# Zero-row keys, transposed vector sums and operand addresses in a two-block transformer kernel

## The chip, the cores and the metric

The kernel runs on one core of a Trainium2 chip. The metric is the device time of one execution in microseconds; for the kernel before it is the median of three runs. Engines are named TensorE (PE in the profile, PEld for its weight loads), VectorE (DVE), ScalarE (ACT), GpSimd (POOL) and SyncE (SP, which issues most DMAs).

## The reference

256 tokens of width 1024 pass through two transformer blocks of two layers each. All arithmetic is float32. Cut to what matters here:

```python
def first_block(x, p, positions, w_in, ...):
    for i in range(2):
        q, k, v, qi, ki, wi, u, vs = split(x @ w_in[i], ...)
        a = dsa_attention(rope(q), rope(k), v, rope(qi), rope(ki), wi)  # 8 heads on 2 key heads of 64
        b = spatial_gating(gelu(u), gelu(vs), ...)
        x = layer_norm(ALPHA * x + concat(a, b) @ w_o[i], ...)
        gate, up = split(x @ w_ffn_in[i], 2)
        ffn = (silu(gate) * up) @ w_ffn_out[i]
        ple = (p[i] @ w_ple[i]) * sigmoid(x @ w_ple_gate[i])
        x = layer_norm(ALPHA * x + ffn + ple, ...)
    return x

def second_block(x, c, positions, ada_w, ada_b, ...):
    cond = silu(c)                                            # one vector of 1024
    for layer in range(2):
        sh1, sc1, g1, sh2, sc2, g2 = split(cond @ ada_w[layer] + ada_b[layer], 6)
        h = rms_norm(x, norm_mix[layer]) * (1 + sc1) + sh1
        # layer 0: MLA (8 heads of 64 + 32) and dilated windows (3 groups of 4 heads of 64)
        # layer 1: differential attention (4 heads of 2 x 64) and MoBA (8 heads of 64)
        x = x + g1 * mixer(h, ...)
        h = rms_norm(x, norm_mlp[layer]) * (1 + sc2) + sh2
        x = x + g2 * (relu(h @ mlp_w1[layer]) ** 2 @ mlp_w2[layer])
    return x
```

In dsa_attention a small index attention (4 heads of 64) chooses which keys of each query row count.

## The kernel before

**Tiling.** The tokens are two halves of 128, numbered rr = 0 and 1, one token to a partition. Weights stream from HBM in units of 128 partitions x 1024 floats. SP issues the loads in order into ring "w" of six buffers (`load_unit`, L396). Each unit is split into a high part h (ScalarE, L407) and the remainder l (VectorE, L408), both in a format of fewer bits, fp32r; a float32 product is then three fp32r matmuls: high by high, high by low, low by high. While the feed-forwards run, the split parts also go into mix, qTa and kTa, tiles that attention uses at other times.

**Three forms of product.** `product` (L436 to L438) keeps a 128x128 block of x stationary and moves 512 columns of weights (384 or 336 in some projections), for one half. `joint_product` (L457 to L459), the first part of the feed-forwards, keeps a 128x128 block of weights stationary and moves 256 columns of x, both halves at once; it has 1,152 matmuls for each of its three lines, 832 of them with weights in the ring and 320 with weights in mix, kTa or qTa. `joint_rows` (L472 to L474), the feed-forwards' second part, keeps blocks of the hidden state (hh and hl, one for each half) stationary and moves 512 columns of weights. The split x lies in XH and XL.

**Scores.** `scores` (L578 to L594) first writes a mask into a PSUM bank with an identity matmul (L587) and adds q times k (L593) for two heads, two instructions to each product, since plain float32 goes through in two. Query and key columns of two heads of 64 lie above each other in one 128-row block, in qTa or qTb and in a key tile: vaa for DSA, kTb for the dilated heads and MoBA, kTa for the differential heads and MLA. A head uses partitions 0 to 63 or 64 to 127 (`lo : lo + 64`) of both. MLA's heads have 96 rows and always begin at partition 0. There are 44 score calls on 64 rows: 16 of DSA, 12 dilated, 8 differential and 8 of MoBA, 208 instructions in the records of TensorE. The DSA index attention has 8 more matmul pairs of 64 rows (L778). Transposed heads come out of PSUM through `columns_of` and its callers, with one copy for up to four blocks, on ScalarE or, at L767, VectorE.

**Conditioning.** `conditioning` (L646) computes cond @ ada_w in 12 jobs. Each streams eight 128x1024 tiles through ring "w"; VectorE multiplies each by a column of cond and adds it up in acc (tag kTb; L656 for the first, L658 for the seven others). The sum over the 128 partitions remains. Four jobs (the gates) get it by a matmul with ones as rows. The other eight, called column jobs here, need it as columns of 128 and take eight float32 matmuls of one column (L676) and an addition (L680). The jobs run as fillers in the feed-forwards, between the joint matmuls.

**Addresses.** A tile's place in SBUF is a byte offset within each partition, given out pool by pool (const, ring, act). What matters below is that offset modulo 256: the ring's w, h and l are at 0, XH and XL at 0, qTa0 and qTa1 at 224, mix0, mix1 and kTa at 32, hid0, hh0 and hl0 at 32, hid1, hh1, hl1 and kTb at 128, hr0 and hr1 (a small input of the first block) at 160 and 224. SBUF is full.

**Order.** The Tile framework puts instructions into each engine's queue by priorities (PRIORITY) and estimated times, so a changed instruction can change the order around it.

Of the kernel before, what the change touches and what calls it, by code (L numbers as in the profile page):

```python
# [10 lines left out]
F32 = mybir.dt.float32  # L11
F32R = mybir.dt.float32r
BF16 = mybir.dt.bfloat16
I32 = mybir.dt.int32
# [8 lines left out]
NH = 2  # L23
# [55 lines left out]
def body(ctx: ExitStack, tc: tile.TileContext, I, out):  # L79
# [8 lines left out]
    act = pool("act", 1)  # L88
    psum = pool("psum", 1, space=bass.MemoryType.PSUM)
# [27 lines left out]
    def new(p, shape, tag, bufs, dt=F32):  # L117
        serial[0] += 1
        return p.tile(shape, dt, tag=tag, name=f"{tag}_{serial[0]}", bufs=bufs)
# [94 lines left out]
    def setup_second():  # L214
# [15 lines left out]
        G.iota(diff_i, pattern=[[-1, P]], base=0, channel_multiplier=1)  # L230
        strided = {}
# [262 lines left out]
    XH = act.tile([P, NH, KB, P], F32, tag="xh", name="xh", bufs=1)  # L494
    XL = act.tile([P, NH, KB, P], F32, tag="xl", name="xl", bufs=1)
# [150 lines left out]
    def conditioning():  # L646

        cond, ones, cols_a = C["cond"], C["ones"], C["cols_a"]
        for l, j in COND_JOBS:
# [23 lines left out]
            else:  # L673
                ps = bank("m", 0)
                for k in range(KB):
                    T.matmul(ps[:, k : k + 1], acc[:, k * P : (k + 1) * P], ones[:, 0:1],  # L676
                             start=True, stop=True)
                bcol = cols_a[:, l * 48 + j * 8 : l * 48 + j * 8 + 8]
                m = ctile([P, KB], f"mod{l}{name}")
                V.tensor_tensor(m, ps[:, :KB], bcol, op=ALU.add)  # L680
# [70 lines left out]

    @ranked("fin")
# [8 lines left out]
    def dsa_select(rr, row, wi, qT, kT, m4):  # L761
# [3 lines left out]
        def put(b0, ps3):  # L765
            A.copy(qT[:, 4:6], ps3[:, 0:2])
            V.tensor_copy(kT[:, 1, rr * P : rr * P + P], ps3[:, 2])  # L767
# [5 lines left out]
        for half in range(2):  # L773
            ps = bank("a", rr)
            p3 = ps[:, : 2 * nk].rearrange("p (h k) -> p h k", h=2)
            lo = half * 64
            for j in range(2):
                T.matmul(p3[:, j], qT[lo : lo + 64, 4 + j], kT[lo : lo + 64, 1, :nk], start=True, stop=True)  # L778
# [19 lines left out]
    def dsa_heads(rr, qT, kT, va, mask, mix):  # L798
        nk = P * (rr + 1)
        for g in range(2):  # L800
            lo = g * 64
            po3 = None
            for j0 in (0, 2):
                p3 = scores([(qT[lo : lo + 64, j0 + j], kT[lo : lo + 64, 0, :nk]) for j in range(2)], rr,
                            [(0, mask)])
# [12 lines left out]
    def first_layer(l, rr):  # L818
        x = state["x"][rr]
        xs = transposed(rr, x, 8, kind="a")  # L820
        kT = params(("kT", l), lambda: new(act, [P, 2, S], "vaa", 1))
# [28 lines left out]
        def put(b0, ps3):  # L850
            if b0:
                A.copy(kT[:, 0, rr * P : rr * P + P], ps3[:, 0])
# [311 lines left out]
    def dilated(rr, rqs, qT, kT, va, mix):  # L1164
        nk = P * (rr + 1)
        for lo_h in range(2):
            lo = lo_h * 64
# [3 lines left out]
            for g in range(3):  # L1171
                far, diag = C["dil_masks"][g]
                masks = [(0, diag)] if rr == 0 else [(0, far), (P, diag)]
                p3 = scores([(qT[lo : lo + 64, 2 * g + h // 2], kT[lo : lo + 64, 2 * g + h // 2, :nk]) for h in hs],
                            rr, masks, "a" if g < 2 else "m")
# [21 lines left out]
    def even_layer(rr):  # L1197
# [14 lines left out]
        dkT = params(("dil_kT",), lambda: new(act, [P, 6, S], "kTb", 1))  # L1212
# [40 lines left out]
        to_columns(rr, dk, 6, dkT[:, :, rr * P : rr * P + P])  # L1253
# [7 lines left out]
    def diff(rr, rqs, qT, kT, va, mix):  # L1261
        nk = P * (rr + 1)
        po3 = None
        for h0 in (0, 2):
            sums = new(act, [P, 2, 2], "df_s", 2)
            pts = []
            for m in range(2):
                lo = m * 64
# [197 lines left out]
```

## Time and profile before

| what | value |
|---|---|
| device time, median of 3 runs (range) | 1335.47 us (1334.87 to 1335.48) |
| profiled execution: time, span of the trace | 1336.68 us, 1335.0 us |
| TensorE busy | 1303.6 us (98%), 8006 instructions |
| VectorE busy | 1011.1 us (76%), 2096 |
| ScalarE busy | 727.2 us (54%), 1488 |
| GpSimd busy | 38.6 us (3%), 99 |
| read from HBM | 267.60 MB, 201 GB/s over the span |

The times are from one execution recorded on the chip. "Busy" is the share of the span in which an engine has at least one instruction in work. Matmuls overlap in this record (each begins before the last one's recorded end), so a matmul's duration is not what it costs; the distance of start times, called its pitch below, is. The chain of waits follows the work that ended last back to what released it.

### The profile page before, as it was taken

Reading aid. Unit: us, or ns where it says so; the run is one execution under the profiler, and the core shown is the slowest. Engines: PE = TensorE matmul, PEld = TensorE weight load, DVE = VectorE, ACT = ScalarE, POOL = GpSimd, SP = SyncE. Lnnn points to the kernel's source line nnn. Section 1 sums busy time; section 2 is a strip of 40 time slices with the busy share of each in tenths; the row PEclk is TensorE's granted clock in tenths of the full one; section 3 lists DMA queues with packets and bytes.
Section 4 is the critical chain, followed back from the end, with each engine's and each line's share of the span. In section 5 each row is a group of like instructions: output and inputs, shape, how many; then the busy total and the mean of one; then the engine's idle time right before and its main releaser. Section 6 shows DMA issues by size and latency. Waiting matters only on the chain.

```text
span 1335.0 us, 21908 instructions
## 1 busy us (share of the span) xinstructions
PE 1303.6 (98%) x8006; PEld 1145.2 (86%) x8006; DVE 1011.1 (76%) x2096; ACT 727.2 (54%) x1488; POOL 38.6 (3%) x99
## 2 busy tenths in 40 slices
PE   7999999999999999999899998999999999999998
PEld 6788999998878799999798976998987777799896
DVE  7979888668878988577769867867677996865552
ACT  6554554343555454454567667655447675854541
POOL 2000000000000000000010000000001000000000
PEclk9999999999999999999999999999999999999999
DMA  8635898786654698587564444777765534565631
GB/s 283 212 128 172 301 325 287 247 292 233 178 174 143 190 330 307 183 304 256 157 167 121 146 154 146 232 238 244 236 232 142 178 111 143 174 203 184 185 107 48
DMA packets 121805, 270.10 MB, mean 202 GB/s; under 512 B 9587, under 2 KB 30160, under 8 KB 121696
## 3 DMA queue, kind: packets, MB, share of 16 engines
q1 hardware_dynamic: 120304, 265.62, 60.8%
q0 software_dynamic: 1392, 3.07, 1.1%
q8 instruction: 63, 1.03, 0.3%
q14 instruction: 46, 0.38, 0.1%
HBM read 267.60 MB, written 1.05 MB: 201 GB/s over the span
## 4 chain that ended last, share of the span: by engine, by line
PE 86%; DVE 7%; ACT 3%; DMA 2%; issue 2%; POOL 1%; SPq 0%; POOLq 0%; ACTq 0%; DVEq 0%
PE m L458 10%; PE m L459 10%; PE m L457 10%; PE m L436 7%; PE m L438 7%; PE m L437 7%; PE a L472 6%; PE a L473 6%; PE a L474 6%; PE a L593 3%; PE a L436 2%; PE a L437 2%; PE a L438 2%; DVE l L408 2%; PE a L628 1%
## 5 line engine op out<-in xcount | busy, mean ns | idle before, releaser
L407 ACT CAST h<-w 128x512 fp32r<-128x512 f32 (+3 forms) x634 | 354.4, 605 | 269.9 <-DMA w<-in_w_ffn_in 51.7
L408 DVE TENSOR_TENSOR l<-w,h 128x512 fp32r<-128x512 f32 (+3 forms) x634 | 401.5, 664 | 74.5 <-ACT h L407 73.7
L457 PE MATMUL m<-xh,h 128*128 128x256 f32 x832 | 235.9, 284 | 0.0
L458 PE MATMUL m<-xl,h 128*128 128x256 f32 x832 | 235.7, 283 | 0.0
L459 PE MATMUL m<-xh,l 128*128 128x256 f32 x832 | 235.5, 283 | 0.0
L436 PE MATMUL m<-h,xh 128*128 128x512 f32 (+3 forms) x544 | 208.2, 384 | 3.5 <-ACT h L407 2.9
L438 PE MATMUL m<-h,xl 128*128 128x512 f32 (+3 forms) x544 | 206.2, 381 | 4.6 <-DVE xl L1020 4.4
L437 PE MATMUL m<-l,xh 128*128 128x512 f32 (+3 forms) x544 | 205.7, 379 | 0.6 <-DVE l L408 0.4
L458 PEld LDWEIGHTS m<-xl,h 128*128 128x128 f32 x832 | 159.0, 191 | 0.4
L457 PEld LDWEIGHTS m<-xh,h 128*128 128x128 f32 x832 | 158.9, 191 | 0.3
L459 PEld LDWEIGHTS m<-xh,l 128*128 128x128 f32 x832 | 158.9, 191 | 0.3
L658 DVE SCALAR_TENSOR_TENSOR kTb<-w,cond,kTb 128x1024 f32<-128x1024 f32 x84 | 107.6, 1280 | 30.8 <-DMA w<-in_ada_w 30.2
L438 PEld LDWEIGHTS m<-h,xl 128*128 128x128 f32 x544 | 103.9, 191 | 20.1 <-DVE xl L1020 5.3
L436 PEld LDWEIGHTS m<-h,xh 128*128 128x128 f32 x544 | 104.4, 192 | 18.5 <-ACT h L407 3.6
L437 PEld LDWEIGHTS m<-l,xh 128*128 128x128 f32 x544 | 104.1, 191 | 14.1 <-DVE l L408 1.6
L472 PE MATMUL a<-h,hh 128*128 128x512 f32 x216 | 85.5, 396 | 0.0
L473 PE MATMUL a<-l,hh 128*128 128x512 f32 x216 | 85.4, 396 | 0.0
L474 PE MATMUL a<-h,hl 128*128 128x512 f32 x216 | 85.4, 395 | 0.0
L407 ACT CAST qTa<-w 128x512 fp32r<-128x512 f32 x60 | 34.4, 622 | 36.6 <-DMA w<-in_w_ffn_in 11.4
L407 ACT CAST kTa<-w 128x512 fp32r<-128x512 f32 x60 | 34.7, 626 | 33.2 <-PE m L459 7.4
L407 ACT CAST mix<-w 128x512 fp32r<-128x512 f32 x60 | 34.7, 620 | 30.7 <-DMA w<-in_w_ffn_in 8.5
L408 DVE TENSOR_TENSOR kTa<-w,kTa 128x512 fp32r<-128x512 f32 x60 | 39.0, 687 | 14.7 <-ACT kTa L407 14.7
(441 smaller groups left out, 2458.3 us busy)
## 6 DMA issues: line engine op xcount, KB each, us to landing
w<-in_mlp_w SPq DMA_DIRECT2D x128, 512.0 KB, 4.2
w<-in_ada_w SPq DMA_DIRECT2D x96, 512.0 KB, 4.8
w<-in_w_ffn_in SPq DMA_DIRECT2D x80, 512.0 KB, 5.1
w<-in_w_ffn_out SPq DMA_DIRECT2D x44, 512.0 KB, 5.4
w<-in_odd_w_in SPq DMA_DIRECT2D x24, 512.0 KB, 4.4
w<-in_even_w_in SPq DMA_DIRECT2D x24, 384.0 KB, 3.4
w<-in_w_in SPq DMA_DIRECT2D x16, 512.0 KB, 7.2
w<-in_w_o SPq DMA_DIRECT2D x16, 512.0 KB, 6.0
```

The source lines that it names most:

```text
L407: split = [A.copy(r(ht[:, c]), wt[:, c]), V.tensor_tensor(r(lt[:, c]), wt[:, c], ht[:, c], op=ALU.subtract)]
L408: V.tensor_tensor(r(lt[:, c]), wt[:, c], ht[:, c], op=ALU.subtract)]
L436: T.matmul(ps, r(xh), r(wh[:, cols]), start=first, stop=False)
L437: T.matmul(ps, r(xh), r(wl[:, cols]), start=False, stop=False)
L438: mm = T.matmul(ps, r(xl), r(wh[:, cols]), start=False, stop=last)
L457: T.matmul(ps, r(wh[:, cols]), r(XH[:, :, k]), start=first, stop=False)
L458: T.matmul(ps, r(wh[:, cols]), r(XL[:, :, k]), start=False, stop=False)
L459: T.matmul(ps, r(wl[:, cols]), r(XH[:, :, k]), start=False, stop=last)
L472: T.matmul(ps, r(xh), r(wh[:, cols]), start=start and k == 0, stop=False)
L473: T.matmul(ps, r(xh), r(wl[:, cols]), start=False, stop=False)
L474: T.matmul(ps, r(xl), r(wh[:, cols]), start=False, stop=False)
L658: V.scalar_tensor_tensor(acc, wt, cond[:, k : k + 1], acc, op0=ALU.mult, op1=ALU.add)
```

## The change

Three things are changed.

**Zero-row keys.** A key tile gets one block for each head instead of one for two heads. Each block holds the head's 64 rows on the partitions where they were and zeros on the other 64 (`zeroed_keys`, two GpSimd memsets for each tile), so q times k takes all 128 rows of both operands: the other head's query rows meet zeros. A key copy from PSUM becomes two, one for the lower and one for the upper 64 partitions (`to_keys`). vaa grows to [128, 4, 256], kTb to [128, 12, 256] for the dilated heads and [128, 8, 256] for MoBA, kTa's key tile to [128, 8, 256]; MLA's stay.

**Turned vector sums.** In a column job VectorE transposes acc in 32x32 blocks into a buffer of ring "w" and reduces each row over groups of 32 to 128x32. One float32 matmul with `quarters` (ones where row and column agree modulo 32) adds up the four groups of partitions, and four additions on 32 partitions each take the place of the one.

**Addresses.** Tiles of pool act whose size is not a multiple of 64 floats, and vaa and vab, go to a new pool "small", and XH and XL go to a new pool "last", behind a tile of 32 bytes. XH and XL then lie at 32 modulo 256, and the ring, hh, hl, hr, hid, mix, qTa and kTa at 0. The scratch for dynamic DMA descriptors shrinks from 16384 to 4096 bytes for each partition, which makes room for the larger tiles.

Context lines are cut to the nearest.

```diff
@@ -86,6 +86,8 @@
     act = pool("act", 1)
+    last = pool("last", 1)
+    small = pool("small", 1)
     psum = pool("psum", 1, space=bass.MemoryType.PSUM)
@@ -116,6 +118,9 @@
         serial[0] += 1
+        if p is act and (math.prod(shape[1:]) % 64 or tag in ("vaa", "vab")):
+            p = small
         return p.tile(shape, dt, tag=tag, name=f"{tag}_{serial[0]}", bufs=bufs)
@@ -228,6 +233,10 @@
         G.iota(diff_i, pattern=[[-1, P]], base=0, channel_multiplier=1)
+        quarters = C["quarters"] = ctile([P, P], "quarters")
+        rem = new(act, [P, P], "hid0", 2, I32)
+        V.tensor_single_scalar(rem, diff_i, 31, op=ALU.bitwise_and)
+        V.tensor_scalar(quarters, rem, 0, 1.0, op0=ALU.is_equal, op1=ALU.mult)
         strided = {}
@@ -491,8 +500,11 @@
-    XH = act.tile([P, NH, KB, P], F32, tag="xh", name="xh", bufs=1)
-    XL = act.tile([P, NH, KB, P], F32, tag="xl", name="xl", bufs=1)
+    apart = last.tile([P, 8], F32, tag="apart", name="apart", bufs=1)
+    V.memset(apart, 0.0)
+    XH = last.tile([P, NH, KB, P], F32, tag="xh", name="xh", bufs=1)
+    XL = last.tile([P, NH, KB, P], F32, tag="xl", name="xl", bufs=1)
@@ -671,13 +683,19 @@
             else:
+                turned = new(ring, [P, UNIT], "w", NW)
+                V.transpose(turned, acc)
+                part = new(act, [P, 32], "ada_q", 1)
+                V.tensor_reduce(out=part, in_=turned.rearrange("p (b k) -> p b k", k=32), op=ALU.add, axis=AX.X)
                 ps = bank("m", 0)
-                for k in range(KB):
-                    T.matmul(ps[:, k : k + 1], acc[:, k * P : (k + 1) * P], ones[:, 0:1],
-                             start=True, stop=True)
+                T.matmul(ps[:, 0:32], C["quarters"], part, start=True, stop=True)
                 bcol = cols_a[:, l * 48 + j * 8 : l * 48 + j * 8 + 8]
                 m = ctile([P, KB], f"mod{l}{name}")
-                V.tensor_tensor(m, ps[:, :KB], bcol, op=ALU.add)
+                for q in range(4):
+                    at_q = slice(32 * q, 32 * q + 32)
+                    V.tensor_tensor(m[at_q], ps[at_q, q:32:4], bcol[at_q], op=ALU.add)
                 if name[:2] == "sc":
@@ -749,6 +767,25 @@
+    def zeroed_keys(shape, tag):
+        kz = new(act, shape, tag, 1)
+        G.memset(kz[64:128, 0::2], 0.0)
+        G.memset(kz[0:64, 1::2], 0.0)
+        return kz
+    def to_keys(rr, row, nblk, kz):
+        here = slice(rr * P, rr * P + P)
+        def put(b0, ps3):
+            n = ps3.shape[1]
+            A.copy(kz[0:64, 2 * b0 : 2 * (b0 + n) : 2, here], ps3[0:64])
+            A.copy(kz[64:128, 2 * b0 + 1 : 2 * (b0 + n) : 2, here], ps3[64:128])
+        columns_of(rr, row, nblk, put)
     @ranked("fin")
@@ -764,7 +801,9 @@
             A.copy(qT[:, 4:6], ps3[:, 0:2])
-            V.tensor_copy(kT[:, 1, rr * P : rr * P + P], ps3[:, 2])
+            here = slice(rr * P, rr * P + P)
+            V.tensor_copy(kT[0:64, 2, here], ps3[0:64, 2])
+            V.tensor_copy(kT[64:128, 3, here], ps3[64:128, 2])
@@ -773,9 +812,8 @@
             p3 = ps[:, : 2 * nk].rearrange("p (h k) -> p h k", h=2)
-            lo = half * 64
             for j in range(2):
-                T.matmul(p3[:, j], qT[lo : lo + 64, 4 + j], kT[lo : lo + 64, 1, :nk], start=True, stop=True)
+                T.matmul(p3[:, j], qT[:, 4 + j], kT[:, 2 + half, :nk], start=True, stop=True)
             A.activation(rel, p3, AF.Relu)
@@ -798,11 +836,9 @@
         for g in range(2):
-            lo = g * 64
             po3 = None
             for j0 in (0, 2):
-                p3 = scores([(qT[lo : lo + 64, j0 + j], kT[lo : lo + 64, 0, :nk]) for j in range(2)], rr,
-                            [(0, mask)])
+                p3 = scores([(qT[:, j0 + j], kT[:, g, :nk]) for j in range(2)], rr, [(0, mask)])
                 nb = softmax_bias(p3, 2, 0.125, None)
@@ -818,7 +854,7 @@
         xs = transposed(rr, x, 8, kind="a")
-        kT = params(("kT", l), lambda: new(act, [P, 2, S], "vaa", 1))
+        kT = params(("kT", l), lambda: zeroed_keys([P, 4, S], "vaa"))
         va = params(("va", l), lambda: new(act, [P, NH, 2, HD + 1], "vab", 1))
@@ -849,7 +885,9 @@
             if b0:
-                A.copy(kT[:, 0, rr * P : rr * P + P], ps3[:, 0])
+                here = slice(rr * P, rr * P + P)
+                A.copy(kT[0:64, 0, here], ps3[0:64, 0])
+                A.copy(kT[64:128, 1, here], ps3[64:128, 0])
             else:
@@ -1164,15 +1202,14 @@
         for lo_h in range(2):
-            lo = lo_h * 64
             hs = (lo_h, lo_h + 2)
                 masks = [(0, diag)] if rr == 0 else [(0, far), (P, diag)]
-                p3 = scores([(qT[lo : lo + 64, 2 * g + h // 2], kT[lo : lo + 64, 2 * g + h // 2, :nk]) for h in hs],
-                            rr, masks, "a" if g < 2 else "m")
+                p3 = scores([(qT[:, 2 * g + h // 2], kT[:, 4 * g + h, :nk]) for h in hs], rr, masks,
+                            "a" if g < 2 else "m")
                 mx = new(act, [P, 8], "mx", 4)[:, :2]
@@ -1209,7 +1246,7 @@
         V.memset(va[:, rr, :, HD : HD + 1], 1.0)
-        dkT = params(("dil_kT",), lambda: new(act, [P, 6, S], "kTb", 1))
+        dkT = params(("dil_kT",), lambda: zeroed_keys([P, 12, S], "kTb"))
         dqT = new(act, [P, 6, P], f"qTb{rr}", 1)
@@ -1250,7 +1287,7 @@
         yield from side
-        to_columns(rr, dk, 6, dkT[:, :, rr * P : rr * P + P])
+        to_keys(rr, dk, 6, dkT)
         into = blocks(rr)
@@ -1265,9 +1302,7 @@
             for m in range(2):
-                lo = m * 64
-                p3 = scores([(qT[lo : lo + 64, h0 + j], kT[lo : lo + 64, h0 + j, :nk]) for j in range(2)], rr,
-                            causal_masks(rr))
+                p3 = scores([(qT[:, h0 + j], kT[:, 2 * (h0 + j) + m, :nk]) for j in range(2)], rr, causal_masks(rr))
                 rq = rqs[:, 2 * h0 + m : 2 * h0 + m + 3 : 2]
@@ -1296,9 +1331,8 @@
             for lo_h in range(2):
-                lo = lo_h * 64
                 b0 = h0 // 2
-                p3 = scores([(qT[lo : lo + 64, b0 + j], kT[lo : lo + 64, b0 + j, :nk]) for j in range(2)], rr,
+                p3 = scores([(qT[:, b0 + j], kT[:, 2 * (b0 + j) + lo_h, :nk]) for j in range(2)], rr,
                             causal_masks(rr))
@@ -1323,11 +1357,10 @@
             ("q1", "moba_q_norm_2", 0, 32), ("k1", "moba_k_norm_2", 0, 32)]))
-        kT_d = params(("diff_kT",), lambda: new(act, [P, 4, S], "kTa", 1))
-        kT_m = params(("moba_kT",), lambda: new(act, [P, 4, S], "kTb", 1))
+        kT_d = params(("diff_kT",), lambda: zeroed_keys([P, 8, S], "kTa"))
+        kT_m = params(("moba_kT",), lambda: zeroed_keys([P, 8, S], "kTb"))
         qT_d = new(act, [P, 4, P], f"qTa{rr}", 1)
         qT_m = new(act, [P, 4, P], f"qTb{rr}", 1)
-        here = slice(rr * P, rr * P + P)
@@ -1338,19 +1371,20 @@
                 rqs[j] = norm_q(rr, heads_view(row, 8), 8, tab)
+                to_columns(rr, row, 4, dst)
             else:
                 norm_k(rr, heads_view(row, 8), 8, tab)
-            to_columns(rr, row, 4, dst)
+                to_keys(rr, row, 4, dst)
         yield from q_or_k(0, True, qT_d)
-        yield from q_or_k(1, False, kT_d[:, :, here])
+        yield from q_or_k(1, False, kT_d)
         ps = bank("m", rr)
         yield from q_or_k(3, True, qT_m, side)
-        yield from q_or_k(4, False, kT_m[:, :, here], side)
+        yield from q_or_k(4, False, kT_m, side)
         ps = bank("m", rr)
@@ -1452,7 +1486,7 @@
-    nc = bacc.Bacc("TRN2", target_bir_lowering=False, num_devices=1)
+    nc = bacc.Bacc("TRN2", target_bir_lowering=False, num_devices=1, dynamic_dma_scratch_size=4096)
     arrays, aps = {}, {}
```

## Rows read from the trace of the kernel before

**Rows 1.** The page: busy times of the engines, and the chain's shares by engine.

```profile
PE 1303.6 (98%) x8006; PEld 1145.2 (86%) x8006; DVE 1011.1 (76%) x2096; ACT 727.2 (54%) x1488; POOL 38.6 (3%) x99
...
PE 86%; DVE 7%; ACT 3%; DMA 2%; issue 2%; POOL 1%; SPq 0%; POOLq 0%; ACTq 0%; DVEq 0%
```

**Rows 2.** Stretches: PE, PEld, DVE, ACT, POOL busy (instructions); PEclk, DMA share, GB/s.

```profile
110.00:335.00 225.00, 225.00 (x1534) 207.62 (x1533) 181.37 (x272) 101.45 (x183) 2.89 (x3) 1.00 0.79 268
700.00:815.00 115.00, 111.94 (x678) 94.95 (x677) 92.06 (x290) 79.09 (x178) 0.00 (x0) 1.00 0.44 132
```

**Rows 3.** TensorE's timeline (start, duration), a DSA score call.

```profile
49.61 0.28 PE L587 MATMUL a<-m,identb 128*128 128x256 bf16 x1
49.82 0.71 PE L593 MATMUL a<-vaa,qTa 64*128 64x128 f32 x4
...
50.80 0.40 PE L437 MATMUL m<-l,xh 128*128 128x512 f32 x1
```

**Rows 4.** The same view, a score call of the MLA heads.

```profile
729.28 0.28 PE L587 MATMUL a<-causal,identb 128*128 128x256 bf16 x1
729.40 0.61 PE L593 MATMUL a<-kTa,qTa 96*128 96x128 f32 x4
729.76 0.43 PE L438 MATMUL m<-h,xl 128*128 128x384 f32 x1
730.03 0.34 PE L436 MATMUL m<-h,xh 128*128 128x384 f32 x1
```

**Rows 5.** The same view, the DSA index heads.

```profile
27.81 1.14 PE L778 MATMUL a<-vaa,qTa 64*128 64x256 f32 x8
28.88 0.44 PE L438 MATMUL m<-h,xl 128*128 128x384 f32 x1
```

**Rows 6.** VectorE's and TensorE's timelines, the end of one column job.

```profile
184.56 1.28 DVE L658 SCALAR_TENSOR_TENSOR kTb<-w,cond,kTb 128x1024 f32<-128x1024 f32 x1
...
206.74 0.27 PE L459 MATMUL m<-xh,qTa 128*128 128x256 f32 x1
...
209.70 0.28 PE L457 MATMUL m<-xh,h 128*128 128x256 f32 x1
```

**Rows 7.** TensorE's timeline, 96 joint matmuls from the ring, 24 from qTa.

```profile
632.31 0.28 PE L457 MATMUL m<-xh,h 128*128 128x256 f32 x1
...
643.71 0.28 PE L459 MATMUL m<-xh,l 128*128 128x256 f32 x1
...
176.85 0.28 PE L457 MATMUL m<-xh,qTa 128*128 128x256 f32 x1
...
179.54 0.28 PE L459 MATMUL m<-xh,qTa 128*128 128x256 f32 x1
```

**Rows 8.** The same, 512 columns: 40 with x, 12 and 12 with hh0.

```profile
458.76 0.39 PE L438 MATMUL m<-h,xl 128*128 128x512 f32 x1
...
467.63 0.40 PE L438 MATMUL m<-h,xl 128*128 128x512 f32 x1
...
922.35 0.40 PE L472 MATMUL a<-h,hh 128*128 128x512 f32 x1
...
924.92 0.39 PE L474 MATMUL a<-h,hl 128*128 128x512 f32 x1
...
259.87 0.39 PE L472 MATMUL a<-kTa,hh 128*128 128x512 f32 x1
...
262.37 0.39 PE L474 MATMUL a<-kTa,hl 128*128 128x512 f32 x1
```

**Rows 9.** Groups by line and form, VectorE: busy, mean ns, idle before, releaser.

```profile
L570 DVE TENSOR_REDUCE nr_v<-rt 128x12 f32<-128x768 f32 x4 | 3.8, 950 | 0.1
```

**Rows 10.** The same view, ScalarE and GpSimd.

```profile
L1089 ACT COPY kTb<-a 128x512 f32<-128x512 f32 x4 | 2.3, 584 | 0.8 <-PE a L749 0.7
...
masks.py:197 POOL MEMSET ident<- 128x128 f32 x1 | 0.2, 205 | 0.3 <-POOLq L1455 0.3
```

**Rows 11.** The page's DMA issues: queue, count, KB each, us to landing.

```profile
w<-in_ada_w SPq DMA_DIRECT2D x96, 512.0 KB, 4.8
```

## The prediction, made before the changed kernel ran

> **What bounds the kernel now.** I read the page first, the span in stretches second, and then single stretches of TensorE's timeline. The page and the chain of waits [rows 1] say the same thing twice: TensorE is busy for 1303.6 us of 1335.0, and 86% of the chain that ended last is TensorE's own work; VectorE holds 7% of it, ScalarE 3%, DMA 2%. The stretches [rows 2] say how firmly. In the first gated feed-forward (110 to 335 us) TensorE is busy for all of 225 us, with VectorE at 181 (81%) and DMA at a share of 0.79. In the MLA and dilated stretch (700 to 815) TensorE is busy for 111.9 of 115, with DMA at 0.44. [...] What shortens the time is therefore a smaller distance from one matmul to the next. "Busy" hides those distances, because matmuls overlap in the record; I read them from start times: the start of the last matmul of a stretch less that of the first, over their number less one.
>
> Times are summed against the profiled execution, 1336.7 us (its span of 1335.0 and 1.7 around it), which lies 1.2 above the median of 1335.47; I take the 1.2 off at the end.
>
> **A. Zero-row keys.** In a score call with keys of 64 rows [rows 3], 1.19 us pass from the start of its mask matmul (49.61) to the start of the second projection matmul behind it (50.80). The call of the MLA heads has the same four q·k instructions on 96 rows, counted from row 0; there the same distance [rows 4] is 729.28 to 730.03, 0.75 us. The matmul inside that distance has 384 columns there and 512 here; by the 512-column pitch (227.4 ns, rows 8) 128 columns are 57 ns, so 0.44 less 0.055 is 0.385 us that the 64-row form costs for each call, on entering, on changing from the lower to the upper partitions of its operand, and on leaving. After the change each call is on 128 rows. I take that, as the nearest row, though 96 rows are not 128, and keep 0.25 (a third less, for calls with something else than a projection behind them) and the undivided 0.44 as ends. Calls: 16 DSA, 12 dilated, 8 differential, 8 MoBA, 44 in all: 44 x 0.385 = 16.9 us (11 to 19).
>
> One thing is lost. The DSA index call [rows 5] has eight 64-row instructions of 256 columns, lower and upper partitions in turn, and its eight take 1.07 us (27.81 to 28.88), 134 ns each. Rows 4 have four of 128 columns in 0.36 (729.40 to 729.76), so eight of twice the columns would take some 1.5 on full rows: the halves run beside each other here. There are four such calls and two short stretches of the differential heads of the same kind; with the entry cost that goes as well I net the loss at 1.2 us in all (0 to 4).
> [...]
> Of 15.7 us I count 0.85 as time, the chain's TensorE share: 13.3 us.
>
> **B. Turned vector sums.** A column job's eight fp32 matmuls with one column (two instructions each) stand between joint matmuls [rows 6]: from the last joint matmul before them (206.74) to the next pair of joint matmuls undisturbed (209.70) pass 2.96 us, with ten joint matmuls inside. At 117.0 ns (rows 7) those are 1.17 us, so the eight pairs cost 1.79, or 0.22 each. The change leaves one pair (32 columns instead of one, which I price the same, 0.2 to 0.4): 1.57 us saved for each of eight jobs, 12.5 us, all in stretches where TensorE is busy throughout [rows 2], so all of it on the path.
> What comes in its place is VectorE's. A transpose of 128x1024 isn't in the trace; the cheapest one-input reduce of 768 is 0.95 us [rows 9], the two-input step of 1024 is 1.28 [rows 6], and I take 1.25 (0.95 to 2.6, twice the step). The reduce of 1024 scales from 0.95 to 1.27. Three additions more are 0.5. That makes 3.0 us a job, 24 in all, some 23 of them in the stretches where VectorE has a quarter to a fifth of its time free. The cover: the job's last VectorE step starts at 184.56 and takes 1.28, and its one-column matmuls come behind 206.74, so TensorE meets the sum about 21 us after it is ready. If that cover is gone, 3 us a job come back.
>
> **C. Layout.** The pitch depends on how the byte offsets of the stationary and the moving operand stand to each other modulo 256. Joint matmuls with weights from the ring (both operands at 0) run at 11.40 us for 95 steps, 120.0 ns [rows 7]; with weights in qTa (at 224, moving x at 0: the moving one 32 ahead) at 2.69 us for 23, 117.0. The change makes the second case of all: weights at 0, x at 32. 2,496 joint matmuls use the ring: x 3.0 = 7.5 us. The 960 in qTa, mix and kTa stay within 1.3 ns of where they are.
> With weights moving, equal is the good case [rows 8]: x stationary at 0 and weights at 0 give 8.87 us for 39, 227.4 ns; hh0 (at 32) with ring weights 2.57 for 11, 233.6; the same hh0 with weights in kTa (at 32 as well) 2.50 for 11, 227.3. The last two share the stationary tile and differ by the moving one's residue. After the change hh, hl, hr and hid are at 0 like the ring: about 1,100 matmuls x 5.5 (hh1 is 5.1 from the good case) = 6.0 us gained. But x as the stationary operand is now 32 off: some 960 matmuls of 512 columns go up to 5.9 ns slower, 5.5 us lost, and 480 of 384 columns up to 6, of which I take half, 1.4 lost. Net 6.6 us gained (0 to 15: nothing if residues don't carry over to other tiles; 15 if x as the stationary operand doesn't mind).
> [...]
>
> **D. What is added elsewhere.** Each key copy from PSUM becomes two on half the partitions, of the same length: 584 ns for four blocks [rows 10], about 5.4 us more on ScalarE, in stretches where it is two thirds busy and TensorE waits little for it; I count 1.5 (0 to 5). Two zeroing memsets for each of five key tiles on GpSimd: the one 128-wide memset takes 205 ns [rows 10], so I put them at 0.5 to 1.4 us each by their 512 to 1536 columns, 9 in all, once per tile and ahead of the first key; GpSimd is 3% busy [rows 1], but its queue carries the rsqrt steps and parameter DMAs, and these come behind the memsets in the odd layer: 0.5 (0 to 4). VectorE's 24 us hold up some weight splits: 1.0 (0 to 6). Sum 3.0.
>
> Sum: 13.3 + 12.5 + 6.6 - 3.0 = 29.4. 1336.7 - 29.4 = 1307.3, less 1.2: **1306 us**.
>
> **The rivals.**
> 1. The layout does nothing, because residues act otherwise than in rows 7 and 8 or the tiles don't land where the title says. For: the pitch is read from tiles that differ in more than their residue. Against: one stationary tile, two residues, 6.2 ns. It gives 1306 + 6.6 = 1313.
> 2. The layout gives more: the joint pitch has room. 256 columns more cost 227.4 - 117.0 = 110.4 ns, so 117.0 can fall to about 110. At 112 all 3,456 joint matmuls give 5.0 ns more, 17 us: 1289. Against: qTa already is the relation that the change makes.
> 3. The weight supply eats the gain in the feed-forward. VectorE goes from 81% to some 92% and the DMA share from 0.79 to 0.84 as TensorE gets faster; the splits of weights then come late, and the joint pitch's 7.5 us and nearly all of part B's 12.5 go into waits: 19 us back, 1325. For: the free share shrinks to under a tenth. Against: no stall of TensorE stands in rows 2 at 81%.
> 4. Slower. The transposed sum takes one of the six load buffers of ring "w", and SP issues the loads in order: each load behind it waits for the reduce. A load lands 4.8 us after its issue [rows 11]. If each of the eight jobs leaves TensorE without weights for that long, 38 us come in against 29 gained: 1346 or so. It decides from 3.7 us a job on the path. Against: VectorE runs 21 us ahead there, and DMA has a fifth of its time free.
> 5. The score calls lose as the index calls do: if two halves ran beside each other there too, 128 rows take away half of each q·k instruction's cover. 208 of them at 0.09 us [rows 4], halved, cost 9.4 us where part A counted 13.3 gained: 1329. For: rows 5. Against: rows 3 against 4, where the 64-row call is the longer one; its lower and upper half are different calls.
>
> **How the numbers follow.** The forecast 0.56, with its own spread from 1296 to 1313 by the ends above. Rival 1 0.16, rival 2 0.09, rival 3 0.10, rival 4 0.04, rival 5 0.02, other costs that leave it within the noise 0.03. The range reaches down to rival 2's upper half, 1290, and up to just short of rival 3, 1323: forecast, rival 1 and a part of 2 and 3 are about 8 in 10. Faster by over 0.2% (2.7 us, about what a measurement of this kernel can tell from no change): the forecast and rivals 1, 2, 3 and 5, 0.93; within it 0.03; slower 0.04.
>
> **What would show it.** A right: score calls with 0.75 us where 1.19 stood, q·k in one form with the rows around it, no 64-row matmul left. B right: one fp32 pair between joint matmuls for each job, and VectorE's additions there not waiting for TensorE; wrong if TensorE waits for the reduce. C right: ring joint pitch 117, hh pitch 227.4, x-stationary 512 pitch about 233; wrong if the first stays at 120 or the last at 227.4. Rival 3 shows as TensorE's idle time before joint matmuls with VectorE or DMA as its releaser, rival 4 as SP's queue waiting for VectorE's reduce. The forecast is wrong most easily if the 96-row call is no fair stand-in for 128 rows, or if what TensorE no longer spends is spent waiting.

## The result and the profile after

The changed kernel takes **1300.63 us** (median of four runs, 1298.29 to 1304.78) where the kernel before takes 1335.47; the ratio is 0.9743, with a 95% interval of 0.9716 to 0.977, so 34 us less (31 to 38). The profiled execution took 1298.29 us, with a span of 1296.6, 38.4 below that of before.

The page of the changed kernel, its busy times and the chain's shares (compare rows 1):

```profile
PE 1267.6 (98%) x7894; PEld 1128.0 (87%) x7894; DVE 1031.1 (80%) x2143; ACT 732.5 (56%) x1500; POOL 47.2 (4%) x109
...
PE 84%; DVE 8%; ACT 3%; DMA 2%; issue 2%; POOL 1%; SPq 0%; POOLq 0%; ACTq 0%; DVEq 0%
```

TensorE still sets the time. It has 112 instructions less, the one-column pairs that went; VectorE has 20.0 us more, ScalarE 5.3, GpSimd 8.6. The same stretches as in rows 2 (first feed-forward; MLA and dilated heads), moved as the span shrank:

```profile
110.00:325.00 215.00, 215.00 (x1474) 198.62 (x1473) 193.69 (x297) 100.40 (x182) 2.96 (x3) 1.00 0.81 278
680.00:790.00 110.00, 106.58 (x676) 93.68 (x677) 91.30 (x287) 79.86 (x179) 0.64 (x1) 1.00 0.45 136
```

In the feed-forward TensorE is busy for all of it with VectorE at 90% (193.69 of 215) and DMA at 0.81. Line numbers have moved: `product` is L445 to L447 now, `joint_product` L466 to L468, `joint_rows` L481 to L483 and q times k L605. TensorE's timeline, the counterparts of rows 3, 6, 7 and 8, first a score call of DSA, then a column job, then 120 joint matmuls from the ring, 48 matmuls with hh or hl and 48 with x stationary:

```profile
56.43 0.27 PE L599 MATMUL a<-m,identb 128*128 128x256 bf16 x1
56.53 0.61 PE L605 MATMUL a<-vaa,qTa 128*128 128x128 f32 x4
56.90 0.47 PE L445 MATMUL m<-h,xh 128*128 128x512 f32 x1
57.21 0.27 PE L640 MATMUL a<-ident,hid 128*128 128x128 f32 x1
...
202.91 0.28 PE L467 MATMUL m<-xl,qTa 128*128 128x256 f32 x1
203.03 0.31 PE L693 MATMUL m<-ada_q,quarters 128*128 128x32 f32 x2
203.17 0.36 PE L468 MATMUL m<-xh,qTa 128*128 128x256 f32 x1
203.37 0.28 PE L466 MATMUL m<-xh,qTa 128*128 128x256 f32 x1
...
578.57 0.28 PE L466 MATMUL m<-xh,h 128*128 128x256 f32 x1
...
592.45 0.28 PE L468 MATMUL m<-xh,l 128*128 128x256 f32 x1
...
869.37 0.39 PE L481 MATMUL a<-h,hh 128*128 128x512 f32 x1
...
880.05 0.39 PE L483 MATMUL a<-h,hl 128*128 128x512 f32 x1
...
1009.87 0.39 PE L445 MATMUL m<-h,xh 128*128 128x512 f32 x1
...
1020.83 0.40 PE L447 MATMUL m<-h,xl 128*128 128x512 f32 x1
```

The call takes 0.78 us from its mask to the second matmul behind it (56.43 to 57.21), where it took 1.19 [rows 3]; in both the matmul in between has 512 columns. The job's pair costs 0.23 us: 0.46 from 202.91 to 203.37, less two joint pitches. The joint pitch is 13.88 us over 119 steps, 116.6 ns (120.0 in rows 7); with hh 10.68 over 47, 227.2 ns (233.6 in rows 8); with x stationary 10.96 over 47, 233.2 ns (227.4 in rows 8).

### The profile page after: what moved, and what is told of

Same layout as the page of the kernel before. It is cut to its first block, busy times and chain, and to the rows that moved or that the text cites. A ratio compares the mean times of both kernels' runs of the same rounds, so it can differ in the third digit from the quotient of the medians.

```text
span 1296.6 us, 21753 instructions
## 1 busy us (share of the span) xinstructions
PE 1267.6 (98%) x7894; PEld 1128.0 (87%) x7894; DVE 1031.1 (80%) x2143; ACT 732.5 (56%) x1500; POOL 47.2 (4%) x109
## 4 chain that ended last, share of the span: by engine, by line
PE 84%; DVE 8%; ACT 3%; DMA 2%; issue 2%; POOL 1%; SPq 0%; POOLq 0%; ACTq 0%; DVEq 0%
PE m L468 10%; PE m L466 10%; PE m L467 10%; PE m L445 7%; PE m L447 7%; PE m L446 7%; PE a L481 6%; PE a L482 6%; PE a L483 6%; PE a L605 2%; PE a L445 2%; PE a L447 1%; PE a L446 1%; DVE l L417 1%; PE a L640 1%
## 5 line engine op out<-in xcount | busy, mean ns | idle before, releaser
L466 PE MATMUL m<-xh,h 128*128 128x256 f32 x832 | 232.5, 280 | 0.0
L468 PE MATMUL m<-xh,l 128*128 128x256 f32 x832 | 232.1, 279 | 0.0
L467 PE MATMUL m<-xl,h 128*128 128x256 f32 x832 | 232.0, 279 | 0.0
L445 PE MATMUL m<-h,xh 128*128 128x512 f32 (+3 forms) x544 | 208.9, 385 | 2.4 <-ACT h L416 1.8
L447 PE MATMUL m<-h,xl 128*128 128x512 f32 (+3 forms) x544 | 206.8, 382 | 4.4 <-DVE xl L1058 4.4
L466 PEld LDWEIGHTS m<-xh,h 128*128 128x128 f32 x832 | 156.4, 188 | 0.4
L467 PEld LDWEIGHTS m<-xl,h 128*128 128x128 f32 x832 | 156.4, 188 | 0.3
L468 PEld LDWEIGHTS m<-xh,l 128*128 128x128 f32 x832 | 156.3, 188 | 0.2
L670 DVE SCALAR_TENSOR_TENSOR kTb<-w,cond,kTb 128x1024 f32<-128x1024 f32 x84 | 107.6, 1281 | 44.5 <-DMA w<-in_ada_w 44.3
L447 PEld LDWEIGHTS m<-h,xl 128*128 128x128 f32 x544 | 103.8, 191 | 18.6 <-DVE xl L1058 5.3
L445 PEld LDWEIGHTS m<-h,xh 128*128 128x128 f32 x544 | 103.9, 191 | 16.2 <-ACT h L416 2.5
L481 PE MATMUL a<-h,hh 128*128 128x512 f32 x216 | 84.4, 391 | 0.0
L483 PE MATMUL a<-h,hl 128*128 128x512 f32 x216 | 84.2, 390 | 0.0
L987 ACT CAST hh<-hid 128x512 fp32r<-128x512 f32 x44 | 27.3, 623 | 61.5 <-PE a L482 48.1
L416 ACT CAST qTa<-w 128x512 fp32r<-128x512 f32 x60 | 34.4, 622 | 33.9 <-DMA w<-in_w_ffn_in 11.8
L483 PEld LDWEIGHTS a<-h,hl 128*128 128x128 f32 x216 | 40.7, 188 | 8.6
```

Of the source, the lines that this page charges most:

```text
L416: split = [A.copy(r(ht[:, c]), wt[:, c]), V.tensor_tensor(r(lt[:, c]), wt[:, c], ht[:, c], op=ALU.subtract)]
L445: T.matmul(ps, r(xh), r(wh[:, cols]), start=first, stop=False)
L447: mm = T.matmul(ps, r(xl), r(wh[:, cols]), start=False, stop=last)
L466: T.matmul(ps, r(wh[:, cols]), r(XH[:, :, k]), start=first, stop=False)
L467: T.matmul(ps, r(wh[:, cols]), r(XL[:, :, k]), start=False, stop=False)
L468: T.matmul(ps, r(wl[:, cols]), r(XH[:, :, k]), start=False, stop=last)
```

## The experiments

Where a mean of a whole class is given below, it is taken from start to start over all fp32r matmuls of the trace of that kernel with the same columns and operands, pauses left out.

First comes each part alone, then the changed kernel without its 32 bytes. The smaller scratch is in all three parts.

**The keys alone** (`zeroed_keys` and `to_keys`; all addresses modulo 256 stay), from the diff:

```diff
-        kT = params(("kT", l), lambda: new(act, [P, 2, S], "vaa", 1))
+        kT = params(("kT", l), lambda: zeroed_keys([P, 4, S], "vaa"))
```

> The zero-row keys alone, addresses modulo 256 as before. Theory (the 64-row form costs TensorE about 0.28 to 0.385 us a score call, and this part is independent of the other two): 12 to 13 us faster, 1322 to 1324 us. Rival (what 128 rows save is lost again, to the index calls that ran side by side and to the doubled key copies on ScalarE): under 9 us faster, above 1326 us, with longer waits of TensorE for key copies.

Measured: 1323.36 us, ratio 0.9907 (0.9889 to 0.9925), 12.4 us less than before. Joint, hh and x pitches are those of before to 0.2 ns. The theory holds.

**The sums alone** (the reduced sums in small tiles of their own, so that no address modulo 256 moves; against the changed kernel):

```diff
-                part = new(act, [P, 32], "ada_q", 1)
+                part = ctile([P, 32], f"part{l}{name}")
```

> The turned vector sums alone, addresses modulo 256 as before. Theory (TensorE loses seven of eight one-column pairs in each of eight jobs and waits for nothing new): 12 us faster, 1322.5 to 1324.5 us, no idle time of TensorE in the feed-forward. Rival (VectorE's 3 us a job and the load buffer taken hold up the weights): 4 to 8 us faster, 1327 to 1331 us, and TensorE waits there for VectorE or a DMA.

Measured: 1324.35 us, ratio 0.9913 (0.9895 to 0.993), 11.6 us less by the ratio. The theory holds; TensorE waits for nothing new in the first feed-forward.

**The addresses alone** (pools "small" and "last", x behind 32 bytes):

> The addresses alone: x at 32 modulo 256, the other operands at 0. Theory as the pitches of the changed kernel give it (joint 119.8 to 116.8 ns on the ring, 118 to 116.7 elsewhere, hh and hl 233 to 227.4, x stationary with 512 columns 229 to 233, 384 columns unchanged): 11 to 12 us faster, about 1324 us. The forecast's own sum: 6.6 us, 1329. Rival (addresses do nothing, and what the changed kernel gains beyond parts one and two comes from another order of the instructions): within 2 us of before, 1334 to 1337 us.

Measured: 1325.97 us, ratio 0.9926 (0.9902 to 0.995), 9.9 us less by the ratio. Addresses alone make the kernel faster; the rival that they do nothing falls, and so does its other order of instructions: TensorE's 8006 matmuls stand in the same order in both traces. By class means the pitches give 12.1 us. One place where the recorded run lost a part of it is the end of the layer-0 feed-forward of the second block, by a wait that the trace of before doesn't have; it is the subject of the last experiments. TensorE's wait there (engine, tile and line <- what ended it: us in total, times, longest), and then the stretch just behind it:

```profile
PE a L441 <- ACT hr L950: 2.0, 1, 2.0
```

```profile
989.00:992.00 3.00, 3.00 (x9) 2.03 (x8) 2.00 (x6) 0.80 (x3) 0.00 (x0) 0.54 0.67 208
```

The granted clock was 0.54 of full speed behind the wait.

The three parts alone sum to 33.9 us, the whole is 34.3: within the intervals they simply add up. An effect of the smaller scratch, which would be counted three times in that sum, has no room beyond the noise.

**The changed kernel with x back at 0:**

```diff
-    apart = last.tile([P, 8], F32, tag="apart", name="apart", bufs=1)
-    V.memset(apart, 0.0)
```

> The changed kernel without the 32 bytes ahead of x, so x and all other operands are at 0 modulo 256. Theory (only the distance of the two operands modulo 256 counts): joint matmuls at 119.8 to 120 ns (3,456 x 3.1 = +10.7 us), x stationary with 512 columns back to 228.9 ns (about 850 x 4.2 = -3.6 us), hh and hl unchanged at 227.4: 7 us slower than the changed kernel, about 1307 us. Rival (the absolute place counts, not the distance): joint pitch stays at 116.8 and the time within 2 us of the changed kernel.

Measured: 1307.59 us, ratio 0.9789 (0.9771 to 0.9807), 6 us slower than the changed kernel by the two ratios. Its timeline, 120 joint matmuls from the ring and 48 with x stationary:

```profile
557.29 0.28 PE L466 MATMUL m<-xh,h 128*128 128x256 f32 x1
...
571.57 0.28 PE L468 MATMUL m<-xh,l 128*128 128x256 f32 x1
...
1017.49 0.40 PE L445 MATMUL m<-h,xh 128*128 128x512 f32 x1
...
1028.19 0.39 PE L447 MATMUL m<-h,xl 128*128 128x512 f32 x1
```

14.28 us over 119 steps are 120.0 ns, 10.70 over 47 are 227.7: with 32 bytes one form wins 3 ns a matmul and the other loses 4 to 5 (233.1 against 228.7 as class means). No instruction of the kernel differs but the memset of those bytes, and the matmuls stand in the same order. The same distance at other places gives the same pitch: before, with qTa at 224 and x at 0, it was 117.0 ns [rows 7]. So in these runs the distance sets the pitch and not the place.

**Other distances.** x at 64 and at 128 modulo 256 (a tile of 64 or 128 bytes ahead of it):

> The changed kernel with x at 64 modulo 256. Theory one (any distance but 0 does for a moving x): joint matmuls at 116 to 117.5 ns. Theory two (the pitch changes with the distance, as 117 at +32 and 118.3 at -32 hint): 118 to 121 ns. x stationary with 512 columns at 233 in both.

> The changed kernel with x at 128 modulo 256. Theory one (any distance but 0): 116 to 117.5 ns for joint matmuls. Theory two (it changes with the distance): 118 to 121 ns. x stationary with 512 columns at 232 to 233 in both, as hh1 was before.

One run each, at 64 first:

```profile
582.43 0.28 PE L466 MATMUL m<-xh,h 128*128 128x256 f32 x1
...
596.44 0.28 PE L468 MATMUL m<-xh,l 128*128 128x256 f32 x1
```

```profile
584.90 0.28 PE L466 MATMUL m<-xh,h 128*128 128x256 f32 x1
...
599.18 0.28 PE L468 MATMUL m<-xh,l 128*128 128x256 f32 x1
```

14.01 us and 14.28 over 119 steps: 117.7 and 120.0 ns here, 117.8 and 119.6 as class means, and 118.3 at -32 (mix and kTa of the kernel before). So theory one falls, that any distance but 0 does: the pitch of a moving x changes with the distance, 119.8 at 0, 116.8 at 32, 117.8 at 64, 119.6 at 128. With x stationary and 512 columns the class means are 233.1, 233.3 and 232.5 at 32, 64 and 128, and 228.7 at 0 only. The single times, 1307.87 and 1315.2 us, can't price a distance: both runs stood still at the place of the last experiments, for 3.7 and 3.3 us.

**Two places for x.** One tile, two views 32 bytes apart, each written and read in its own phase:

```diff
+    XHT = last.tile([P, NH, KB * P + 64], F32, tag="xh", name="xh", bufs=1)
+    XH, XL = x_view(XHT, 8), x_view(XLT, 8)
+    XH0, XL0 = x_view(XHT, 0), x_view(XLT, 0)
```

> The changed kernel once more, on the chip of the three runs beside it, as what they are compared with: 1298 to 1303 us.

> The changed kernel with x kept in one tile under two views: at 0 modulo 256 while only products with x as the stationary operand read it (attention, its output projections), at 32 in the feed-forwards, where the joint matmuls move it. Theory (the distance of the operands counts, for each matmul by itself): joint matmuls stay at 116.8 ns, some 640 of the 930 matmuls of 512 columns with x stationary fall from 233.1 to 228.9 ns, 2.7 us: about 2.5 us faster than the changed kernel beside it. Rival (what a matmul of 512 columns loses is hidden by waits in the attention stretches): no difference that can be measured, with the pitch lower all the same.

Measured: the changed kernel 1301.97 us, ratio 0.9745 (0.9723 to 0.9767); with two views 1302.61, ratio 0.9749 (0.9736 to 0.9762). No gain is to be seen. The pitch did fall (562 of the matmuls with x stationary from 233.1 to 229.0 ns, 2.3 us), so the rival's outcome came. The runs of both kernels lie further apart than 2.3 us, but the traces, with the same matmuls in the same order, bear the rival out stretch by stretch. Between 1000 and 1115 us the matmuls with x stationary gain 1.0 us from start to start, and the stretch takes 114.9 us in both kernels; from 680 to 800 it is 119.7 in both. TensorE's idle time between 1000 and 1115 goes from 1.0 to 1.4 us, and the rest of the gain goes into other distances there, so the shorter pitch doesn't shorten the stretch.

**The load buffer** of the transposed sum:

```diff
-                turned = new(ring, [P, UNIT], "w", NW)
+                turned = new(small, [P, UNIT], "turned", 1)
```

> The changed kernel with the transposed sum in a tile of its own, not in one of the six load buffers. Theory (SP's wait for the reduce, 11.8 us in eight times, is hidden, since VectorE runs ahead): within 1.5 us of the changed kernel, though SP no longer waits for the reduce. Rival (the taken load buffer is what makes the changed kernel's runs differ and costs it weights): 3 us or more faster, and runs closer together.

Measured: 1304.77 us, ratio 0.9768 (0.9747 to 0.979), not faster. In the changed kernel SP waited for the reduce, eight times:

```profile
SPq L144 <- DVE ada_q L690: 11.8, 8, 2.6
```

With a tile of its own this wait is gone, and nothing is won. The run isn't a clean test, since TensorE now stands still twice in the first block's feed-forwards, where the changed kernel's trace has no such wait:

```profile
PE m L466 <- DVE hid L1007: 1.8, 1, 1.8
PE m L466 <- DVE mod0sh L698: 1.7, 1, 1.7
```

That the wait was hidden rests on the changed kernel itself: TensorE is busy for all 215 us of the first feed-forward, while SP waits for the reduce. The rival falls, in its second half too: the four runs still lie 8 us apart (1301.48 to 1309.77).

**The index heads on 64 rows again:**

```diff
-                T.matmul(p3[:, j], qT[:, 4 + j], kT[:, 2 + half, :nk], start=True, stop=True)
+                T.matmul(p3[:, j], qT[lo : lo + 64, 4 + j], kT[lo : lo + 64, 2 + half, :nk], start=True, stop=True)
```

> The changed kernel with the index heads' eight calls back on 64 rows (lower and upper partitions in turn). Theory (the two halves run beside each other): eight instructions of 256 columns take about 1.1 us where the changed kernel has 1.54; in all 0.5 to 1 us less. Rival (full rows are no slower here): 1.5 us or more for the eight.

One run. The eight instructions of 256 columns in the first layer, first in the changed kernel and then in this one:

```profile
28.33 1.89 PE L816 MATMUL a<-vaa,qTa 128*128 128x256 f32 x8
29.87 0.53 PE L446 MATMUL m<-l,xh 128*128 128x384 f32 x1
```

```profile
30.94 1.14 PE L817 MATMUL a<-vaa,qTa 64*128 64x256 f32 x8
32.01 0.44 PE L446 MATMUL m<-l,xh 128*128 128x384 f32 x1
```

From the first to the next matmul of another kind it is 1.54 us on full rows and 1.07 on half rows; over the index calls of both layers 0.56 us are won. By the single start times of the same call in the trace of before [rows 5], also 1.07 us long, the half rows come in pairs 13 ns apart, behind the first pair one pair every 216 ns; the full rows of the changed kernel start one every 216. Counted from the matmul ahead of a call to the second behind it, the two calls of 256 columns win 0.74 us and the two of 128 columns lose 0.35, so 0.39 are left. The theory holds for the calls of 256 columns, and it is a small thing. The single time, 1307.81, can't be read for it: this run stood still for 4 us at the place of the next experiment.

**Why the runs lie 6 to 8 us apart.** The changed kernel's eight runs go from 1297.93 to 1306.34. In the second recorded one TensorE waits at 965, and then runs more slowly. TensorE's timeline, and then the stretch at 968 to 972:

```profile
965.05 0.39 PE L447 MATMUL a<-h,hl 128*128 128x512 f32 x1
966.75 0.50 PE L445 MATMUL a<-qTa,hr 128*128 128x512 f32 x1 [1.32 <-ACT hr L980]
...
969.92 0.63 PE L447 MATMUL a<-h,hr 128*128 128x512 f32 x1
970.35 0.63 PE L445 MATMUL a<-h,hr 128*128 128x512 f32 x1
```

```profile
968.00:972.00 4.00, 4.00 (x11) 3.15 (x12) 1.54 (x5) 0.21 (x1) 0.00 (x0) 0.58 0.77 249
```

The granted clock of that stretch is 0.58 of full speed in the mean, and a matmul of 512 columns takes 0.43 us in it (969.92 to 970.35), where it took 0.23 ahead of the wait (964.82 to 965.05). The wait itself ends with ScalarE's split of the last hidden state (hr), and that waited for VectorE. VectorE's timeline ahead of it:

```profile
953.92 1.28 DVE L670 SCALAR_TENSOR_TENSOR kTb<-w,cond,kTb 128x1024 f32<-128x1024 f32 x1 [1.59 <-DMA w<-in_ada_w]
...
959.43 1.28 DVE L670 SCALAR_TENSOR_TENSOR kTb<-w,cond,kTb 128x1024 f32<-128x1024 f32 x1 [1.22 <-DMA w<-in_ada_w]
...
963.17 2.49 DVE L417 TENSOR_TENSOR l<-w,h 128x512 fp32r<-128x512 f32 x4
965.58 0.68 DVE L1025 TENSOR_TENSOR hid<-hid 128x512 f32<-128x512 f32 x1
```

VectorE stands still twice, 1.59 and 1.22 us, for tiles of conditioning weights whose sum is needed only one layer later; behind these stand the weight splits, and behind those the square (L1025) for which TensorE waits. The same kernel stood there for 0.7 us in its first recorded run, and for some 4 us with the index heads on 64 rows.

The two recorded runs of the changed kernel have the same matmuls in the same order, and their spans differ by 5.3 us. The stretch from 960 to 1000 is 4.3 us longer in the second, and the first 80 us are 2.6 longer; from 800 to 820 it is the first that is 1.6 longer, with a fall of the clock of its own (0.66 from 805 to 810). So this place is the largest part of the difference and not all of it.

A paced conditioning takes the waits away from there:

```diff
-            goal = 81 + 26 * within(spans[2]) // (spans[2][1] - spans[2][0])
+            goal = 81 + min(26, 32 * within(spans[2]) // (spans[2][1] - spans[2][0]))
```

> The changed kernel with the last 26 conditioning steps paced to end at four fifths of the layer-0 feed-forward of the second block and not at its end. [...] Rival (the same loads in less time starve the joint matmuls): slower, with stops of TensorE earlier in that feed-forward.

Measured: **1297.08 us**, runs from 1295.44 to 1297.64, ratio 0.9709 (0.9695 to 0.9723), with the changed kernel at 0.9743 and 0.9745: 4 to 5 us faster than the changed kernel by these ratios, with five runs inside 2.2 us. It ran on another chip than the changed kernel's second set of runs, each against the kernel before on its own chip; all five of its runs lie below the fastest of the changed kernel's eight. TensorE's waits between 940 and 1000 us, the changed kernel first and then the paced one:

```profile
PE a L1051 <- DVE hr L1048: 2.5, 1, 2.5
PE a L445 <- ACT hr L980: 1.3, 1, 1.3
PE a L447 <- DVE hr L981: 0.4, 1, 0.4
```

```profile
PE a L1051 <- DVE hr L1048: 1.6, 1, 1.6
```

The wait for hr (L980, L981) is gone, and with it the fall of the clock (1.00 from 955 to 965, with TensorE busy throughout); so the wait came from the pace of the conditioning and not from the chain of relu, square and split. This is the best of the kernels measured, with the next one level with it.

> The paced kernel with x in two views as well. Theory: both gains add up, 2 to 3 us below the paced kernel, 1294 to 1298 us.

Measured: 1297.18 us, ratio 0.9707 (0.9691 to 0.9723). The two views add nothing that can be measured here either. In the recorded run the wait of L1051, where the next layer's normalization has to end first, was 2.3 us (L1057 there) instead of 1.6, and the clock fell behind it:

```profile
990.00:993.00 3.00, 3.00 (x12) 2.61 (x11) 3.00 (x7) 2.52 (x8) 0.00 (x0) 0.50 0.60 234
```

That is one way in which 2 us get lost again; one recorded run doesn't show that it is what happened in the others.

## Why the prediction was right, and which terms were off

The forecast was 1306 us, a gain of 29.4; measured were 1300.6 and 34, inside the range of 1290 to 1323.

**A, the keys.** Forecast 13.3 less 2.0 for copies and memsets, 11.3; alone they brought 12.4. A call went from 1.19 to 0.78 us, 0.41 against the 0.385 taken from the MLA row, so a 96-row call was a fair stand-in for 128 rows. The single start times of the two calls show where it lay: 0.21 us on entering the 64-row form and 0.19 on leaving it, while the q·k instructions in between follow each other at 112 ns in both. The lost overlap of the index calls was put at 1.2 us, two short stretches of the differential heads included; putting the index calls back gave 0.4 to 0.6. The rival that the score calls lose as the index calls do is out: full rows were faster there. Calls that alternate between the halves took 1.07 us against 1.54 on full rows (the rows at 30.94 and 28.33); a score call stays on one half, and its q·k starts lie 112 ns apart in both forms.

**B, the sums.** Forecast 12.5 less 1.0, 11.5; measured 11.6. The pair cost 0.23 us (0.22 forecast). The transpose, unseen before, took 1.24 us and the reduce 1.22 (1.25 and 1.27 forecast):

```profile
L688 DVE STREAM_TRANSPOSE w<-kTb 128x1024 f32<-128x1024 f32 x8 | 9.9, 1242 | 0.1
L690 DVE TENSOR_REDUCE ada_q<-w 128x32 f32<-128x1024 f32 x8 | 9.7, 1216 | 0.1
```

The cover held as described: one reduce starts at 189.08, and TensorE takes it up at 203.03.

**C, the addresses, is the step that was mis-sized**: 6.6 us forecast, 9.9 measured, 12.1 by the pitches of its trace. By term, each class's change of mean pitch times its matmuls: the ring's joint matmuls brought 7.7 (7.5 forecast) and hh, hl and hr 7.0 (6.0). With x stationary and 512 columns the loss was at most 4.0, not 5.5: the forecast priced the 960 matmuls by the fastest stretch of before (227.4 ns, rows 8), while their class mean there is 228.9, and 233.1 after. In the attention stretches even this loss is not paid in full, as the two views showed. The 384-column matmuls lost nothing (174.5 before, 174.1 after) where 1.4 was set down, and the joint matmuls from mix, kTa and qTa gained 1.1 that was counted as nothing. The upper bound named for this part, 15, held all of it.
The rival that addresses do nothing is out: x at 0, 32, 64 and 128 gave joint pitches of 119.8, 116.8, 117.8 and 119.6 ns.
The rival of a better joint pitch (112 ns) didn't come either: 116.6 is about what qTa had shown (117.0).

**D, the added work**, was put at 3.0. The key copies cost TensorE nothing new, where 1.5 was set down: one wait in the whole trace, 0.2 us, and the trace of before has one of 0.2 like it (the changed kernel first):

```profile
PE a L605 <- ACT kTb L784: 0.2, 1, 0.2
...
PE a L593 <- ACT kTb L1089: 0.2, 1, 0.2
```

The memsets took 0.5 to 1.4 us each, as forecast, and no wait of TensorE names GpSimd.

**The rivals on supply.** That VectorE's load eats the feed-forward's gain didn't come: VectorE rose to 90% (92% forecast), and TensorE has no stop there. That the taken load buffer makes the kernel slower is out: SP's wait was 1.5 us a job, below the 3.7 from which it would decide, and TensorE never stood still for it. (The price named for that rival, 1346, is 1344 by its own sum of 1306 and 38.)
What the forecast overlooked stands elsewhere. In the layer-0 feed-forward of the second block VectorE waits about as long for tiles of conditioning weights before as after (27.6 and 27.9 us in all at the accumulating steps, L658 and L670), but in the shorter feed-forward this wait reaches TensorE, for 0.7 us in one recorded run and 1.7 in the other. With the addresses alone, where VectorE has no work added, it was 2.0 us; the paced kernel's VectorE waits 20.0 and TensorE doesn't. This is a large part of why eight runs of the same kernel differ by 8 us, and why a change of pace alone gave 4 to 5; what makes it longer in one run than in another isn't shown.
The forecast counted nothing for the clock, which is at 1.00 in both stretches of rows 2. The trace of before stands at 0.51 of full speed from 667 to 674 us and at 0.52 from 1022 to 1025.5, so falls of the clock were there to be found.

## What to carry to other kernels

Read the distance of start times by class of operands, not busy time: on a TensorE that is 98% busy nearly a third of this gain (9.9 of 34 us) came from where tiles lie. Price a class by its mean over the whole trace, not by its cleanest stretch, and count it as time only where the stretch itself gets shorter. And when a stretch gets shorter, look at what was paced by it: here VectorE's waits of 1.59 and 1.22 us for tiles that weren't urgent were passed on to what stood behind them, and TensorE stood still for 1.32.

## What the runs showed of the hardware

- In these runs the pitch of a matmul changed with the distance of its operands' addresses modulo 256 bytes. With 512 moving columns and fp32r, as here throughout, equal residues gave 227 to 229 ns, against 232 to 234 at 32, 64 and 128. With 256 moving columns equal residues gave 119.8 ns, x 128 ahead 119.6, 64 ahead 117.8 and 32 ahead, the lowest seen, 116.8. Why the two forms go opposite ways isn't shown.
- Behind waits of TensorE of 1.3, 2.0 and 2.3 us the granted clock was 0.58, 0.54 and 0.50 of full speed in the mean of the stretch just behind (the changed kernel's second recorded run, the addresses alone, the paced kernel with two views), and in the first of these a 512-column matmul took 0.43 us instead of 0.23. Behind a wait of 2.5 us (L1051) it stayed at 1.00 in the changed kernel's first recorded run and was 0.50 in its second (997 to 999 us). What decides isn't shown.
- Four 64-row fp32 matmuls (eight instructions) on alternating halves of the partitions overlapped: 1.07 us against 1.54 on full rows, with starts in pairs 13 ns apart [rows 5]. Around a DSA score call on one half, entering the 64-row form cost 0.21 us and leaving it 0.19.
